# Turning m and x1 to features with 32x32 transposes on VectorE in place of TensorE transposes

## The chip, the cores and the metric

The kernel runs on one core of a Trainium2 chip. Its time is the device time of one execution in microseconds (us). The engines are named as in the profile: PE is TensorE (matmul), PEld its weight load, DVE is VectorE, ACT is ScalarE, POOL is GpSimd, and SP is SyncE, which only issues transfers here. Each engine works through a queue of its own in order; waits between engines go through semaphores.

## What is computed

The reference is one layer of a hybrid decoder block over 256 tokens with 2048 features, in float32. Cut to what matters here:

```python
h = rmsnorm(x, norm_mix_g)
u = h @ w_in                     # 12288 columns, split into ten fields
ya = ...                         # short convolution branch, from four fields
yb = ...                         # HGRN2 branch, from four fields
m = sigmoid(ga) * (ya @ w_a_out) + sigmoid(gb) * (yb @ w_b_out)
x = x + m @ w_o                  # called x1 below
gate = sigmoid(rmsnorm(x, ple_norm_g) @ w_ple_gate)
x = x + gate * (p @ w_ple_proj)
return rmsnorm(x, final_norm_g)
```

## The kernel before

**Products.** Every matrix product is made of steps. A step takes 256 rows of a weight for 512 output columns. It has 2 row blocks, 2 halves of 128 tokens, and 3 matmuls for each (lines 805 to 807): both operands are split into a rounded part (`hi`) and the rest (`lo`), and `hi*hi + hi*lo + lo*hi` is summed in PSUM. The operand with the tokens is stationary, so it must lie with its features on the partitions, and the result comes out with the tokens on the partitions. A result that feeds the next product must therefore be turned, from tokens on the partitions to features on the partitions. That is done for `m` and for `x1`, among others.

**Weights.** SP loads a weight tile `raw` of 128x2048, good for two steps, into one of three buffers (line 105). For each step ScalarE rounds it into `whi` (line 118), and VectorE writes the rest into `wlo` (line 119). Four pairs of `whi` and `wlo` exist until the last groups, and the program splits three steps ahead (`LEAD = 3`).

**Groups and their order.** A group is one block of 512 output columns. The order is: 16 groups of the branch fields; then for j = 0 to 3 the groups `ga`, `gb` (8 steps each), `A`, `B` (4 steps each); then `O` for j = 0 to 3 (8 steps each), called O0 to O3 below; then for j = 0 to 3 `PP` (1 step) and `PG` (8 steps). `mT` is the operand of `O`, `x1T` that of `PG`, and both are read in the order of their feature blocks, so that the blocks of j = 3 are needed in steps 6 and 7 of the group.

**Epilogues.** What follows a group is a generator. It is advanced once after each step, so that a `yield` moves what comes after it behind the next step in program order. The build then orders each engine's queue by its own planning, so that the queues differ somewhat from the program order. For this document:

- `ep_bb` (lines 543 to 557) ends a `B` group. VectorE multiplies `gb` by the PSUM result (line 547), POOL adds `ga` (line 548), and two steps later TensorE turns the 128x1024 tile in eight 128x128 transposes into two PSUM banks (`transposed`, lines 170 to 184). A step later ScalarE copies the banks to `mT`'s `hi` (line 556), and VectorE writes its `lo`, `ml` in the profile (line 557).
- `ep_o` (lines 559 to 591) ends an `O` group. VectorE adds the result to `xs`, the residual (line 564), ScalarE sums squares (line 565), TensorE turns the four feature blocks (line 576), and `put` (lines 147 to 157) writes `x1T`'s `hi` on ScalarE (line 154) and `lo`, `xl` in the profile, on VectorE (line 155).

**Memory.** `t4()` gives a tile of 128x1024 from a ring of eight or five buffers in the temporary pool of the phase: `tmp1`, then `tmp2` from the first `ga` on, then `tmp3`. `third_part` (lines 764 to 785) runs in group O0, after its sixth step: it closes `tmp2` and the pool of the branch results, opens `tmp3` in their place, and has SP load `xs` (line 772, two transfers), the final gain (line 775) and `pT` (line 778). A transfer into the new pool waits for the last use of what lay there. VectorE and ScalarE split `pT` in the same phase (lines 781 and 782, `pl`).

Of the kernel before, what the change touches and what calls it, by code (L numbers as in the profile page):

```python
# [10 lines left out]
F32 = mybir.dt.float32  # L11
F32R = mybir.dt.float32r
AF = mybir.ActivationFunctionType
ALU = mybir.AluOpType
PSUM = bass.MemoryType.PSUM

P = 128
T = 256
NT = T // P
# [5 lines left out]
CW = 512  # L25
# [14 lines left out]
PRM_GMIX, PRM_GPLE, PRM_GHG, PRM_LB, PRM_CONV = 0, 16, 32, 40, 48  # L40
# [5 lines left out]
def hybrid_kernel(ctx, tc, xT, x, pT, prm, gfin, masks, w_in, w_a, w_b, w_o, w_pg, w_pp, out):  # L46
    nc = tc.nc
# [22 lines left out]
    state = {"tmp": "tmp1"}  # L70
# [3 lines left out]
    def nm(s):  # L74
        uid[0] += 1
        return f"{s}_{uid[0]}"

    def t4(tag="t4", bufs=None):
        bufs = bufs or {"tmp1": 8, "tmp2": 5, "tmp3": 5}[state["tmp"]]
        return pools[state["tmp"]].tile([P, 1024], F32, tag=tag, bufs=bufs, name=nm(tag))  # L80

    def bank(tag):
        return ps.tile([P, CW], F32, tag=tag, bufs=4, name=nm(tag))

    def sc(n, tag="sc", bufs=12):
        return small.tile([P, n], F32, tag=tag, bufs=bufs, name=nm(tag))
# [39 lines left out]
    ident = const.tile([P, P], F32, name="ident")  # L126
# [13 lines left out]
    def gain(base, k):  # L140
        return prm_t[:, base + k : base + k + 1]
# [5 lines left out]
    def put(op, k, src, scale=None):  # L147

        hi, lo = op[0][:, k, :], op[1][:, k, :]
        if scale is None:  # L150
            nc.scalar.activation(out=hi, in_=src, func=AF.Copy)
            nc.vector.tensor_tensor(out=lo, in0=src, in1=hi.bitcast(F32), op=ALU.subtract)
        else:
            nc.scalar.activation(out=hi, in_=src, func=AF.Identity, scale=scale)
            nc.vector.scalar_tensor_tensor(
                out=lo, in0=src, scalar=scale, in1=hi.bitcast(F32), op0=ALU.mult, op1=ALU.subtract
            )


    def rsqrt_of(ss, n, width, tag):  # L160

        v = sc(n, tag + "v", 2)
        nc.vector.tensor_scalar(
            out=v, in0=ss, scalar1=1.0 / width, scalar2=EPS, op0=ALU.mult, op1=ALU.add
        )
        r = sc(n, tag + "r", 2)
        nc.gpsimd.tensor_tensor(out=r, in0=v, in1=mhalf[:, :n], op=ALU.pow)
        return r

    def transposed(src):  # L170

        banks = []
        for half in range(2):
            b = bank("s")
            for i in range(2):
                c = half * 2 + i
                for t in range(NT):
                    nc.tensor.transpose(  # L178
                        b[:, i * T + t * P : i * T + (t + 1) * P],
                        src[:, t * CW + c * P : t * CW + (c + 1) * P],  # L180
                        ident,
                    )
            banks.append(b)
        return banks


    def scaled(psum, dst):
# [26 lines left out]
    def ep_f(j, psum):  # L214
        fl = t4()
        scaled(psum, fl)
        yield
        bk = transposed(fl)
        yield
        sg, sn = t4(), t4()  # L220
# [43 lines left out]
    def ep_q(j, psum):  # L264
        sg, qt = t4(), t4()
        sig(psum, sg)
        times(psum, sg, qt)
        yield
        yield
        bk = transposed(qt)  # L270
        yield
        qT = t4("qT", 1)
        for h in range(2):
            nc.vector.tensor_copy(out=qT[:, h * 512 : (h + 1) * 512], in_=bk[h])
        state["qT", j] = qT
# [16 lines left out]
    def hgrn(j):  # L292
# [161 lines left out]
        yield  # L454
        yield
        bk = transposed(yb)
        yield
        for h in range(2):
# [84 lines left out]
    def ep_bb(j, psum):  # L543
        ga, gb = state["ga", j], state["gb", j]
        for t in range(NT):
            s = slice(t * CW, (t + 1) * CW)
            nc.vector.tensor_tensor(out=gb[:, s], in0=gb[:, s], in1=psum[t], op=ALU.mult)  # L547
        nc.gpsimd.tensor_tensor(out=gb, in0=ga, in1=gb, op=ALU.add)  # L548
        yield
        yield  # L550
        bk = transposed(gb)
        yield
        for h in range(2):
            k = j * 4 + h * 2
            hi, lo = (x[:, k : k + 2, :].rearrange("p k t -> p (k t)") for x in state["mT"])
            nc.scalar.activation(out=hi, in_=bk[h], func=AF.Copy)
            nc.vector.tensor_tensor(out=lo, in0=bk[h], in1=hi.bitcast(F32), op=ALU.subtract)

    def ep_o(j, psum):
        xs = state["x"]  # L560
        src = t4()
        for t in range(NT):
            d = xs[:, t, j * CW : (j + 1) * CW]
            nc.vector.tensor_tensor(out=d, in0=d, in1=psum[t], op=ALU.add)
            nc.scalar.activation(
                out=src[:, t * CW : (t + 1) * CW], in_=d, func=AF.Square,
                accum_out=state["ss2"][:, t * 4 + j : t * 4 + j + 1],
            )
        yield
        bk = []  # L570
        for half in range(2):
            b = bank("s")
            for i in range(2):
                c = j * 4 + half * 2 + i
                for t in range(NT):
                    nc.tensor.transpose(  # L576
                        b[:, i * T + t * P : i * T + (t + 1) * P], xs[:, t, c * P : (c + 1) * P], ident
                    )
            bk.append(b)
        yield  # L580
        for h in range(2):
            for i in range(2):
                k = j * 4 + h * 2 + i
                put(state["x1T"], k, bk[h][:, i * T : (i + 1) * T], gain(PRM_GPLE, k))
        if j == 3:
            tot = sc(2, "tot2", 1)
            nc.vector.tensor_reduce(
                out=tot, in_=state["ss2"].rearrange("p (t j) -> p t j", t=NT),
                axis=mybir.AxisListType.X, op=ALU.add,
            )  # L590
            state["rstd2"] = rsqrt_of(tot, NT, D, "r2")
# [64 lines left out]
    def ep_last(t, halves):  # L656
# [7 lines left out]
    epilogues = {  # L664
        "f": ep_f, "q": ep_q, "iv": ep_iv, "og": ep_og, "c": ep_c, "xa": ep_xa, "za": ep_za, "b": ep_b,
        "ga": ep_ga, "gb": ep_gb, "A": ep_a, "B": ep_bb, "O": ep_o, "PG": ep_pg, "PP": ep_pp,
    }
    groups = []
# [22 lines left out]
    for c in range(KT // 2):  # L691
        n = 2 * (c % 2)
        nc.sync.dma_start(
            out=xraw[c // 2].rearrange("p (k t) -> p k t", k=4)[:, n : n + 2, :],
            in_=xT[:, 2 * c : 2 * c + 2, :],
# [116 lines left out]
    for pos, (gi, c) in enumerate(steps[:last_group]):  # L812
        kind, j, w, g, opname = groups[gi]
# [25 lines left out]
        hi, lo = parts.pop(pos)  # L839
        for i in range(2):  # L840
            k = 2 * c + i
            s = slice(i * CW, (i + 1) * CW)
# [25 lines left out]
    for t, halves in ((0, (0, 1)), (1, (0,)), (1, (1,))):  # L868
        bk, n = bank("g"), CW // 2
        for c in range(nlast):  # L870
# [3 lines left out]
            hi, lo = parts[last_group + c]  # L874
            for i in range(2):
                k = 2 * c + i
                s = slice(i * CW + halves[0] * n, i * CW + (halves[-1] + 1) * n)
# [83 lines left out]
```

## Time and profile before

| what | value |
|---|---|
| median of 3 runs | 852.69 us (852.5 to 853.07) |
| the profiled execution | 852.66 us, of which its span is 850.9 us |
| granted TensorE clock in it | 0.998 |
| busy: PE, DVE, ACT, POOL | 839.6, 527.2, 425.0, 82.8 us |
| transferred | 164.12 MB, mean 193 GB/s |

How to read the rows. A row of a timeline has the start, the duration, the engine, the line, the operation, `out<-in`, the count of merged instructions, and in brackets how long the engine sat idle before it and what ended that. A row of a group has the count behind `x`, then the busy time in us and the mean duration in ns, then the idle time in front and its releasers. In the chain of waits a row has the start, the duration, the engine, the tile and the line. Matmuls are pipelined, so each shows 0.39 us but a new one starts every 0.227 us, and a busy PE isn't a PE at its peak. Times in the text are us unless ns is said.

### The profile page before, as it was taken

The numbers are of one execution on the slowest core, as the hardware profiler recorded it, in microseconds if no ns is written. First come the engines' busy times: TensorE is split into PE (matmuls) and PEld (weight loads), VectorE is DVE, ScalarE is ACT, GpSimd is POOL, SyncE is SP. The second block draws the span as 40 slices with busy tenths as digits, with TensorE's granted clock in tenths as the row PEclk, the third lists the DMA queues.
The fourth block names the chain that finished last, engine by engine and source line by source line (L and its number), as shares of the span: only waits on it lengthen the run. The fifth ranks groups of instructions, "written<-read, shape, count | busy, mean of one in ns | idle before, by whom it ended". The sixth has DMA issues, their size and how long they took to land.

```text
span 850.9 us, 9907 instructions
## 1 busy us (share of the span) xinstructions
PE 839.6 (99%) x3897; PEld 697.8 (82%) x3897; DVE 527.2 (62%) x611; ACT 425.0 (50%) x514; POOL 82.8 (10%) x76
## 2 busy tenths in 40 slices
PE   9999999999999999999999999999999999999995
PEld 6788888888888888888888888888888888888885
DVE  7484686977674587968446446446446555556572
ACT  7854664434644754534443444444444554455553
POOL 1010042202010042101001001001001000001110
PEclk9999999999999999999999999999999999999999
DMA  9865464444555455444555555555555955554542
GB/s 340 335 215 184 158 223 162 171 174 155 191 199 177 169 198 178 169 165 174 169 191 191 198 197 199 171 193 188 190 198 173 362 181 186 184 196 165 197 149 99
DMA packets 25966, 164.12 MB, mean 193 GB/s; under 512 B 3008, under 2 KB 3008, under 8 KB 7744
## 3 DMA queue, kind: packets, MB, share of 16 engines
q1 hardware_dynamic: 25488, 162.93, 53.8%
q8 instruction: 30, 0.49, 0.2%
q10 hardware_dynamic: 432, 0.56, 0.2%
q14 instruction: 16, 0.13, 0.0%
HBM read 161.39 MB, written 2.10 MB: 192 GB/s over the span
## 4 chain that ended last, share of the span: by engine, by line
PE 96%; issue 1%; DMA 1%; ACT 1%; DVE 0%; SPq 0%; POOLq 0%; POOL 0%; ACTq 0%
PE g L806 31%; PE g L807 31%; PE g L805 31%; PE s L310 1%; PE s L178 1%; DMA raw<-in_w_in 1%; PE s L418 0%; PE s L576 0%; PE s L430 0%; PE s L431 0%; PE s L429 0%; ACT whi L118 0%; ACT xs L647 0%; ACT t L630 0%; SPq L700 0%
## 5 line engine op out<-in xcount | busy, mean ns | idle before, releaser
L119 DVE TENSOR_TENSOR wlo<-raw,whi 128x1024 fp32r<-128x1024 f32 (+1 forms) x294 | 372.6, 1273 | 270.6 <-ACT whi L118 270.0
L118 ACT ACTIVATE whi<-raw 128x1024 fp32r<-128x1024 f32 (+1 forms) x294 | 308.6, 1053 | 361.9 <-PE g L807 354.4
L805 PE MATMUL g<-whi,xh 128*128 128x512 f32 (+1 forms) x912 | 354.5, 389 | 0.9 <-ACT whi L118 0.9
L806 PE MATMUL g<-wlo,xh 128*128 128x512 f32 (+1 forms) x912 | 352.0, 386 | 0.2 <-DVE wlo L119 0.2
L807 PE MATMUL g<-whi,xl 128*128 128x512 f32 (+1 forms) x912 | 351.8, 386 | 0.0
L805 PEld LDWEIGHTS g<-whi,xh 128*128 128x128 f32 x912 | 171.5, 188 | 35.5 <-ACT whi L118 2.3
L806 PEld LDWEIGHTS g<-wlo,xh 128*128 128x128 f32 x912 | 171.5, 188 | 34.8 <-DVE wlo L119 1.2
L807 PEld LDWEIGHTS g<-whi,xl 128*128 128x128 f32 x912 | 171.4, 188 | 34.4
L805 PE MATMUL g<-whi,mh 128*128 128x512 f32 x128 | 50.2, 392 | 0.0
L807 PE MATMUL g<-whi,ml 128*128 128x512 f32 x128 | 49.9, 390 | 0.0
L806 PE MATMUL g<-wlo,mh 128*128 128x512 f32 x128 | 49.8, 389 | 0.0
L548 POOL TENSOR_TENSOR gb<-ga,gb 128x1024 f32<-128x1024 f32 x4 | 9.6, 2396 | 258.3 <-DVE gb L547 258.3
L807 PEld LDWEIGHTS g<-whi,ml 128*128 128x128 f32 x128 | 24.0, 188 | 5.1
L806 PEld LDWEIGHTS g<-wlo,mh 128*128 128x128 f32 x128 | 24.0, 188 | 4.9
L805 PEld LDWEIGHTS g<-whi,mh 128*128 128x128 f32 x128 | 24.0, 188 | 4.8
L338 POOL TENSOR_TENSOR X<-t,kT 128x256 f32<-128x256 f32 x12 | 11.5, 956 | 168.3 <-ACT t L352 115.4
L805 PE MATMUL g<-whi,yaTh 128*128 128x512 f32 x64 | 24.9, 389 | 0.0
L806 PE MATMUL g<-wlo,yaTh 128*128 128x512 f32 x64 | 24.9, 389 | 0.0
L807 PE MATMUL g<-whi,yaTl 128*128 128x512 f32 x64 | 24.9, 389 | 0.0
L805 PE MATMUL g<-whi,ybTh 128*128 128x512 f32 x64 | 24.9, 389 | 0.0
L806 PE MATMUL g<-wlo,ybTh 128*128 128x512 f32 x64 | 24.9, 389 | 0.0
L807 PE MATMUL g<-whi,ybTl 128*128 128x512 f32 x64 | 24.9, 389 | 0.0
(153 smaller groups left out, 559.1 us busy)
## 6 DMA issues: line engine op xcount, KB each, us to landing
raw<-in_w_in SPq DMA_DIRECT2D x91, 1024.0 KB, 4.8
raw<-in_w_o SPq DMA_DIRECT2D x16, 1024.0 KB, 4.8
raw<-in_w_pg SPq DMA_DIRECT2D x16, 1024.0 KB, 4.7
raw<-in_w_a SPq DMA_DIRECT2D x8, 1024.0 KB, 5.0
raw<-in_w_b SPq DMA_DIRECT2D x8, 1024.0 KB, 5.0
raw<-in_w_in SPq DMA_DIRECT2D x9, 512.0 KB, 7.8
t<-in_xT SPq DMA_DIRECT2D x8, 256.0 KB, 7.0
t<-in_x SPq DMA_DIRECT2D x4, 512.0 KB, 8.7
```

Of the source, the lines that this page charges most:

```text
L118: nc.scalar.activation(out=hi[:, s], in_=src[:, s], func=AF.Copy)
L119: nc.vector.tensor_tensor(out=lo[:, s], in0=src[:, s], in1=hi[:, s].bitcast(F32), op=ALU.subtract)
L178: nc.tensor.transpose(b[:, i * T + t * P : i * T + (t + 1) * P], src[:, t * CW + c * P : t * CW + (c + 1) * P], ident,)
L310: nc.tensor.matmul(bk[:, s], X[:, 0, h, :], X[:, 1, h, :], start=True, stop=True)
L338: eng.tensor_tensor(out=xv[:, w, :, :, half, :], in0=ev[:, :, blk, :, half, :], in1=src[:, :, blk, :, half, :], op=ALU.mult,)
L548: nc.gpsimd.tensor_tensor(out=gb, in0=ga, in1=gb, op=ALU.add)
L805: nc.tensor.matmul(psum, oh, hi, start=first, stop=False)
L806: nc.tensor.matmul(psum, oh, lo, start=False, stop=False)
L807: nc.tensor.matmul(psum, ol, hi, start=False, stop=last)
```

## The change

VectorE can transpose blocks of 32x32 inside 32 partitions, and may write them to another quarter of the partitions. A new helper `turned` makes the whole turn of a 128x1024 tile in 16 such instructions, one for each pair of a source quarter `a` and a destination quarter `b`. Each handles 32 partitions and 2x4x32 elements. It yields after every `step` of them, 4 in general and 8 for the last x1 block. The result goes to an SBUF tile of the `t4` ring, not to PSUM, and the copies that follow read it there: for `m` one copy and one subtraction of 1024 columns in place of two of 512. The `tmp2` pool, which held only `ga` and `gb`, now holds the ring too.

```diff
+    def turned(src, dst, step):
...
+        s = src.rearrange("p t (c b e) -> p t c b e", b=4, e=32)
+        d = dst.rearrange("p c (t a e) -> p t c a e", t=NT, e=32)
+        for n in range(16):
+            a, b = n % 4, n // 4
+            nc.vector.transpose(
+                out=d[32 * b : 32 * b + 32, :, :, a, :], in_=s[32 * a : 32 * a + 32, :, :, b, :]
+            )
+            if n % step == step - 1:
+                yield
...
         nc.gpsimd.tensor_tensor(out=gb, in0=ga, in1=gb, op=ALU.add)
         yield
-        yield
-        bk = transposed(gb)
-        yield
-        for h in range(2):
-            k = j * 4 + h * 2
-            hi, lo = (x[:, k : k + 2, :].rearrange("p k t -> p (k t)") for x in state["mT"])
-            nc.scalar.activation(out=hi, in_=bk[h], func=AF.Copy)
-            nc.vector.tensor_tensor(out=lo, in0=bk[h], in1=hi.bitcast(F32), op=ALU.subtract)
+        m = t4()
+        yield from turned(
+            gb.rearrange("p (t n) -> p t n", t=NT), m.rearrange("p (c n) -> p c n", c=4), 4
+        )
+        k = j * 4
+        hi, lo = (x[:, k : k + 4, :].rearrange("p k t -> p (k t)") for x in state["mT"])
+        nc.scalar.activation(out=hi, in_=m, func=AF.Copy)
+        nc.vector.tensor_tensor(out=lo, in0=m, in1=hi.bitcast(F32), op=ALU.subtract)
...
         yield
-        bk = []
-        for half in range(2):
-            b = bank("s")
-            for i in range(2):
-                c = j * 4 + half * 2 + i
-                for t in range(NT):
-                    nc.tensor.transpose(
-                        b[:, i * T + t * P : i * T + (t + 1) * P], xs[:, t, c * P : (c + 1) * P], ident
-                    )
-            bk.append(b)
-        yield
-        for h in range(2):
-            for i in range(2):
-                k = j * 4 + h * 2 + i
-                put(state["x1T"], k, bk[h][:, i * T : (i + 1) * T], gain(PRM_GPLE, k))
+        x1 = t4()
+        yield from turned(xs[:, :, j * CW : (j + 1) * CW], x1.rearrange("p (c n) -> p c n", c=4), 8 if j == 3 else 4)
+        for c in range(4):
+            put(state["x1T"], j * 4 + c, x1[:, c * T : (c + 1) * T], gain(PRM_GPLE, j * 4 + c))
```

## The prediction

> **What bounds the kernel now.** I read the busy shares and the chain of waits first, then the groups of instructions.
>
> ```profile
> span 850.9 us, 9907 instructions
> PE 839.6 (99%) x3897; PEld 697.8 (82%) x3897; DVE 527.2 (62%) x611; ACT 425.0 (50%) x514; POOL 82.8 (10%) x76
> PE 96%; issue 1%; DMA 1%; ACT 1%; DVE 0%; SPq 0%; POOLq 0%; POOL 0%; ACTq 0%
> L119 DVE TENSOR_TENSOR wlo<-raw,whi 128x1024 fp32r<-128x1024 f32 (+1 forms) x294 | 372.6, 1273 | 270.6 <-ACT whi L118 270.0
> L118 ACT ACTIVATE whi<-raw 128x1024 fp32r<-128x1024 f32 (+1 forms) x294 | 308.6, 1053 | 361.9 <-PE g L807 354.4
> ```
>
> TensorE is 96% of the chain. VectorE waits for ScalarE, and ScalarE waits for TensorE to give a weight buffer back. So whatever leaves TensorE shortens the run, as long as VectorE's `wlo` stays ahead of the matmuls.
>
> The PE timeline around the first transposes of `gb` gives the rhythm.
>
> ```profile
> 453.31 0.39 PE L805 MATMUL g<-whi,xh 128*128 128x512 f32 x1
> 456.03 0.39 PE L805 MATMUL g<-whi,xh 128*128 128x512 f32 x1
> 458.76 1.04 PE L178 MATMUL s<-ident,gb 128*128 128x128 f32 x8
> 459.55 0.47 PE L805 MATMUL g<-whi,xh 128*128 128x512 f32 x1
> 462.39 0.39 PE L805 MATMUL g<-whi,xh 128*128 128x512 f32 x1
> ```
>
> A step (256 weight rows, 12 matmuls) takes 456.03 - 453.31 = 2.72. From 456.03 to 462.39 there are two steps and eight transposes: 6.36 - 5.44 = 0.92 for one block of eight. The chain of waits lists eight such blocks, first and last here:
>
> ```profile
> 458.92 0.87 PE s L178 x8
> ...
> 745.56 0.87 PE s L576 x8
> ```
>
> **The change part by part.** Removed: 64 TensorE transposes in 8 blocks, all on the chain: 8 x 0.92 = 7.4 us.
>
> Added: 128 VectorE transposes of 32 partitions x 256 elements (2x4x32), 16 per block. No row shows one. The nearest rows are instructions with 256 elements per partition, and for the far end the scan:
>
> ```profile
> L234 DVE TENSOR_SCALAR kT<-t,lc 128x256 f32<-128x256 f32 x8 | 2.7, 346 | 0.0
> L408 DVE TENSOR_TENSOR kT<-kT,t 128x256 f32<-128x256 f32 x4 | 1.7, 416 | 0.0
> L155 DVE SCALAR_TENSOR_TENSOR xl<-s,prm_t,xh 128x256 fp32r<-128x256 f32 x16 | 7.1, 479 | 0.6 <-ACT xh L154 0.3
> 679.83 0.87 DVE L155 SCALAR_TENSOR_TENSOR xl<-s,prm_t,xh 128x256 fp32r<-128x256 f32 x2
> L253 DVE TENSOR_TENSOR_SCAN b<-carry,t 128x1024 f32<-128x1024 f32 x2 | 4.6, 2284 | 0.0
> ```
>
> Lower end: two L155 take 0.87 for 2 x 0.479, so neighbours overlap by 0.09; 0.45 less that is 0.36. Upper end, a transpose that moves as slowly as the scan: L408 and the 1.23 of `wlo` (below) give 1.06 ns per element and 0.145 fixed, so the scan needs (2284 - 145) / 1024 = 2.09 ns per element, and 256 elements 0.68. I take T = 0.45 without overlap, between L408 and L155: one pass of 256 elements with a little to fill. The range keeps 0.36 and 0.68.
>
> The rows show overlap only between instructions on all 128 partitions. The Trainium skill (VectorE: DVE Perf Modes, Two Vector instructions with no wait between them) says that an instruction whose input or output starts in another quarter of the partitions than the one before is held until all earlier ones have finished, and here the input quarter changes every time; with overlap the total would be 845.3, held 846.8 (both below), and no row can show which. The same page (The three transpose paths) gives 311 ns for a 128x128 bf16 VectorE transpose; 128 elements more at 0.96 GHz make an estimate of 0.44, and by it 846.5.
>
> Now, does VectorE stay ahead? The first block, with 0 at 453.31:
>
> ```profile
> 453.51 1.06 ACT L118 ACTIVATE whi<-raw 128x1024 fp32r<-128x1024 f32 x1 [1.66 <-PE g L807]
> 453.02 1.28 DVE L547 TENSOR_TENSOR gb<-gb,g 128x512 f32<-128x512 f32 x2
> 454.38 2.39 POOL L548 TENSOR_TENSOR gb<-ga,gb 128x1024 f32<-128x1024 f32 x1 [66.76 <-DVE gb L547]
> 454.60 3.25 DVE L119 TENSOR_TENSOR wlo<-raw,whi 128x1024 fp32r<-128x1024 f32 x1 [0.30 <-ACT whi L118]
> 460.05 1.23 DVE L119 TENSOR_TENSOR wlo<-raw,whi 128x1024 fp32r<-128x1024 f32 x1 [1.06 <-ACT whi L118]
> 461.19 1.28 DVE L557 TENSOR_TENSOR ml<-s,mh 128x512 fp32r<-128x512 f32 x2
> 466.41 1.23 DVE L119 TENSOR_TENSOR wlo<-raw,whi 128x1024 fp32r<-128x1024 f32 x1 [1.49 <-ACT whi L118]
> ```
>
> Weights have four buffers, so the `wlo` made at 454.60 is read three steps later, at 3 x 2.72 + 0.23 = 8.39; the k-th after it at 8.39 + 2.72k. Per step VectorE has 1.49 idle, which hides three transposes. The changed program's queue runs wlo0, 5T, wlo1, 5T, wlo2, 5T, wlo3, T, wlo4, ml. The first transpose waits for POOL's add (end 3.46), but wlo0 already ends at 4.54, because it takes 3.25 beside that add; nothing is queued behind the wait that is not covered. With 1.25 per `wlo`: wlo1 ends at 8.05 (due 11.1), wlo2 at 11.55 (due 13.8), wlo3 at 15.05 (due 16.55), wlo4 at 16.75 (due 19.3), ml at 18.0. Least spare: 1.5. No stall. If the cover went, each 0.1 of T would cost 1.5 a block.
>
> The copies cost nothing: the two L557 of 1.28 become one of some 1.25, two ScalarE copies become one of 1.06 like `whi`, and the scalings of x1 read SBUF, where ScalarE's form takes 494 ns against 468:
>
> ```profile
> L154 ACT ACTIVATE xh<-t,prm_t 128x256 fp32r<-128x256 f32 x16 | 7.2, 494 | 0.3 <-DMA t<-in_xT 0.3
> L154 ACT ACTIVATE xh<-s,prm_t 128x256 fp32r<-128x256 f32 x16 | 6.8, 468 | 3.8 <-DVE xl L155 3.8
> ```
>
> ScalarE's 1.66 idle per step hides it.
>
> Moved: the load of x for the residual (L772). It goes where `tmp2` lay, and `tmp2` now holds `m`. In the changed queue it stands behind two more loads of `w_o`, the second of which waits for wlo4, and it waits itself for the last `ml`. Before:
>
> ```profile
> 651.93 0.39 PE L805 MATMUL g<-whi,mh 128*128 128x512 f32 x1
> 656.95 1.61 SPq L772 DMA_DIRECT2D xs<-in_x  x2
> DMA to landing us min/median/max: 8.1/8.7/9.4
> 659.08 0.43 SPq L778 DMA_DIRECT2D t<-in_pT  x1
> DMA to landing us min/median/max: 11.6/11.6/11.6
> 674.19 0.69 DVE L564 TENSOR_TENSOR xs<-xs,g 128x512 f32<-128x512 f32 x1 [1.90 <-issue]
> 673.27 1.06 ACT L118 ACTIVATE whi<-raw 128x1024 fp32r<-128x1024 f32 x1 [1.93 <-DMA raw<-in_w_o]
> DMA to landing us min/median/max: 3.2/4.8/13.2
> ```
>
> (The three landing rows are of x, of pT, and of all weight loads.) With 0 at O's first matmul (651.93), x was issued at 5.0 and landed 9.3 later, well before its first use at 674.19 - 651.93 - 0.92 = 21.3. Now it is issued at 18.0 (ml, above). The `w_o` load ahead of it leaves 1.25 earlier than x, so I take a landing at 26.9 (26.4 to 27.3): 5.6 too late, and VectorE waits in front of its queue: add, wlo8, add, wlo9, 8T, pl, wlo10, 5T, wlo11, 3T, wlo12, four xl, wlo13. From 26.9, an add 0.6: wlo8 28.75 (due 30.15), wlo9 30.6 (32.87), 8T 34.2, pl 34.8 (pT lands at 18.0 + 2.1 + 11.6 = 31.7), wlo10 36.05 (due 35.59, late 0.46), wlo11 39.55 (due 38.31, late 1.24), wlo12 42.15 (due 42.27 by then), xl 44.05, wlo13 45.3 (due 44.99): 0.31 more. TensorE stalls 1.24 + 0.31 = 1.55 here, once. The loads queued behind x shift with it: the first weight load after it was in at 673.27, 16.3 after x's issue, so now at 34.3, and its `whi` at 35.4, ahead of wlo11's start at 38.3; gfin is first read in the last phase.
>
> The other x1 blocks have x. Group O3, whose queue holds T, wlo0, 7T, wlo1, 8T, wlo2, four xl, wlo3:
>
> ```profile
> 742.39 1.28 DVE L564 TENSOR_TENSOR xs<-xs,g 128x512 f32<-128x512 f32 x2
> 743.97 1.23 DVE L119 TENSOR_TENSOR wlo<-raw,whi 128x1024 fp32r<-128x1024 f32 x1 [0.30 <-ACT whi L118]
> ```
>
> The adds end 1.0 after its last step: wlo0 2.7, wlo1 7.1 (due 11.1), wlo2 11.95 (13.8), wlo3 15.15 (16.55): 1.4 to spare; x1 is read six steps into PG0, after PP0's one, at 19. O1 and O2, with a `wlo` in every five transposes, keep 3.8.
>
> Sum against the profiled execution's own 852.66 us (1.76 outside the span; the median is 852.69): 852.66 - 7.4 + 1.55 = 846.8.
>
> **The rivals.**
>
> Full gain: T 0.36 by overlap, or x early by 1.6: the stall goes (1.55 - 31 x 0.09 is below nothing) and 845.3 follows. For it: L155's overlap. Against: no row has it across quarters.
>
> Slower: VectorE becomes the bound, because a float32 transpose costs two passes, like the scan. At T = 0.68 each of four m blocks loses 15 x 0.23 - 1.5 = 1.95, the O0 block 1.55 + 31 x 0.23 - 1.95 = 6.7 (B3's own loss pays part), O3 16 x 0.23 - 1.4 = 2.3, O1 and O2 nothing: 16.8 - 7.4 = +9.4, 862.1. It decides from T = 0.58, where m loses 4 x 0.45, O0 5.1 and O3 0.7, 7.6 in all. For it: no transposing instruction is in the trace; against: every plain 256-element row is at most 0.48.
>
> No change: x lands 13.2 after issue, as the latest weight load did, at 31.2: 4.3 more on a `wlo` that is late already. 846.8 + 4.3 = 851.1. For it: gfin, pT and weights share the queue; against: x's own 9.4.
>
> **How the numbers follow.** Forecast 0.50 (T from 0.41 to 0.54: 846 to 850), full gain 0.16, no change 0.07, slower 0.27. This kernel's runs tell 0.2% (1.7 us) from no change, so faster 0.66, same 0.07, slower 0.27. The range 845 to 858 goes up to T = 0.63 and leaves out the upper part of the slower case, towards 862.1.
>
> **What would show it.** A transpose row of 0.4 to 0.5 starting where the last one ends; no idle PE time in ga, gb, A and B steps; the x adds waiting for their load in O0, then some 1.5 of PE waiting for `wlo` in O1; PE's last matmul some 6 us earlier. Wrong if a transpose takes over 0.58, if PE waits in the m blocks, or if x's issue stays near 5.

## The result, and the profile after

| | us, median | range |
|---|---|---|
| before | 852.66 | 852.5 to 853.07 |
| after | 847.41 | 847.35 to 847.55 |

The ratio is 0.9938 [0.9919, 0.9958]: 0.6% faster, 5.25 us. One more execution of the changed kernel took 4834.85 us, with its 128x512 matmuls 1.28 to 1.46 us apart at a granted clock of 1.00, for a reason that isn't known, and the profile of that set fell on it; so the profile read here is that of a second set of the same kernel (847.24, 846.72 to 847.41; its profiled execution 846.72, the fastest of the four).

First the page of the changed kernel: the span, the busy times, the chain of waits by engine, and the two groups that prepare the weights.

```profile
span 844.9 us, 9887 instructions
PE 832.2 (98%) x3833; PEld 690.6 (82%) x3833; DVE 580.4 (69%) x735; ACT 423.8 (50%) x510; POOL 86.0 (10%) x76
PE 94%; DVE 2%; issue 2%; DMA 1%; ACT 1%; SPq 0%; POOLq 0%; POOL 0%; ACTq 0%
L119 DVE TENSOR_TENSOR wlo<-raw,whi 128x1024 fp32r<-128x1024 f32 (+1 forms) x294 | 371.6, 1272 | 207.1 <-ACT whi L118 205.5
L118 ACT ACTIVATE whi<-raw 128x1024 fp32r<-128x1024 f32 (+1 forms) x294 | 307.4, 1052 | 330.8 <-PE g L812 315.7
```

PE is busy 7.4 less, and DVE 53.2 more, which came out of its idle time in front of `wlo` (270.6 before, 207.1 now). But the chain shows something new: DVE holds 2% of it, where it had 0%. So somewhere TensorE waited for VectorE. The groups of transposes and a DVE timeline of the block behind B0 come next.

```profile
L196 DVE STREAM_TRANSPOSE t<-xs 32x256 f32<-32x256 f32 x64 | 27.9, 436 | 1.1
L196 DVE STREAM_TRANSPOSE t<-gb 32x256 f32<-32x256 f32 x64 | 27.9, 436 | 1.0
```

```profile
454.30 3.25 DVE L119 TENSOR_TENSOR wlo<-raw,whi 128x1024 fp32r<-128x1024 f32 x1 [0.30 <-ACT whi L118]
457.48 2.22 DVE L196 STREAM_TRANSPOSE t<-gb 32x256 f32<-32x256 f32 x5
459.73 1.22 DVE L119 TENSOR_TENSOR wlo<-raw,whi 128x1024 fp32r<-128x1024 f32 x1
460.99 2.23 DVE L196 STREAM_TRANSPOSE t<-gb 32x256 f32<-32x256 f32 x5
...
469.67 1.23 DVE L573 TENSOR_TENSOR ml<-t,mh 128x1024 fp32r<-128x1024 f32 x1
```

A transpose takes 436 ns, and five in a row 2.22: (2.22 - 0.436) / 4 = 0.446 from start to start, so none begins before the last one ends. VectorE has no idle time left in the block. Where TensorE waited is found with the busy time of PE by stretches (start to end, length, PE busy, matmuls, granted clock, DMA share and GB/s): the first three rows hold the first three `m` blocks, the fourth is O0, the fifth O1, and the sixth holds O2, O3 and most of the `PP` and `PG` groups.

```profile
452.00:520.00 68.00, 68.00 (x302) 1.00 0.57 199
520.00:580.00 60.00, 60.00 (x267) 1.00 0.56 193
580.00:640.00 60.00, 60.00 (x266) 1.00 0.56 193
648.85:671.94 23.09, 22.31 (x97) 1.00 0.53 192
671.94:693.70 21.76, 21.76 (x97) 1.00 0.78 302
693.70:820.00 126.30, 126.30 (x559) 1.00 0.54 194
```

PE idles in O0 alone. Before, it had no idle time there either, eight transposes included:

```profile
651.93:674.60 22.67, 22.67 (x105) 1.00 0.80 313
```

After, PE's timeline in O0, and VectorE's:

```profile
664.94 0.39 PE L812 MATMUL g<-whi,ml 128*128 128x512 f32 x1
665.54 0.50 PE L810 MATMUL g<-whi,mh 128*128 128x512 f32 x1 [0.21 <-ACT mh L572]
665.88 0.40 PE L811 MATMUL g<-wlo,mh 128*128 128x512 f32 x1
666.84 0.50 PE L812 MATMUL g<-whi,ml 128*128 128x512 f32 x1 [0.57 <-DVE ml L573]
667.18 0.40 PE L810 MATMUL g<-whi,mh 128*128 128x512 f32 x1
```

```profile
663.95 0.44 DVE L196 STREAM_TRANSPOSE t<-gb 32x256 f32<-32x256 f32 x1
664.42 1.23 DVE L119 TENSOR_TENSOR wlo<-raw,whi 128x1024 fp32r<-128x1024 f32 x1
665.57 1.22 DVE L573 TENSOR_TENSOR ml<-t,mh 128x1024 fp32r<-128x1024 f32 x1
666.70 2.35 DVE L119 TENSOR_TENSOR wlo<-raw,whi 128x1024 fp32r<-128x1024 f32 x2
670.58 1.22 DVE L119 TENSOR_TENSOR wlo<-raw,whi 128x1024 fp32r<-128x1024 f32 x1 [1.52 <-ACT whi L118]
674.25 0.69 DVE L580 TENSOR_TENSOR xs<-xs,g 128x512 f32<-128x512 f32 x1 [2.45 <-DMA xs<-in_x]
...
676.72 0.69 DVE L580 TENSOR_TENSOR xs<-xs,g 128x512 f32<-128x512 f32 x1 [0.65 <-DMA xs<-in_x]
677.33 1.22 DVE L119 TENSOR_TENSOR wlo<-raw,whi 128x1024 fp32r<-128x1024 f32 x1
```

And SP's, where the load of x is issued:

```profile
666.87 0.80 SPq L777 DMA_DIRECT2D xs<-in_x  x2
```

The matmuls that wait are the first of O0's step 6, which reads the last `m` block. The last transpose ends at 664.39, and step 6 was due at 665.17; `mh` came a little late and `ml` at 666.79. The starts in these rows are 0.60, 0.34, 0.96 and 0.34 apart in place of 0.227: 2.24 - 0.91 = 1.33 lost. The load of x came out as the forecast had it, issued 18.0 after O0's first matmul (666.87 - 648.85), and the adds wait for it; but O1, which was to pay, has no idle PE at all.

The profiled pair agrees with that: 852.66 - 7.36 + 1.33 = 846.63, and 846.72 was measured. Two other differences cancel in this. The profiled execution was 0.30 ahead before the first changed instruction (`wlo` at 454.30, before at 454.60), and its end behind PE's last matmul is 0.36 longer (844.9 - 835.67 against 850.9 - 842.03). A stretch that holds neither is the one from O0's first matmul to PE's last: 186.82, before 190.10, so 3.28 less. Five of the eight blocks lay in it, and 5 x 0.92 - 1.33 = 3.27.

### The profile page after: what moved, and what is told of

It reads as the page before. It is cut to its first block, busy times and chain, and to the rows that moved or that the text cites. A ratio compares the mean times of both kernels' runs of the same rounds, so it can differ in the third digit from the quotient of the medians.

```text
span 4833.0 us, 9887 instructions
## 1 busy us (share of the span) xinstructions
PE 4822.6 (100%) x3833; PEld 3387.5 (70%) x3833; DVE 583.7 (12%) x735; ACT 427.7 (9%) x510; POOL 77.2 (2%) x76
## 4 chain that ended last, share of the span: by engine, by line
PE 98%; issue 1%; ACT 0%; DVE 0%; POOLq 0%; POOL 0%
PE g L810 32%; PE g L812 31%; PE g L811 31%; PE s L326 2%; PE s L178 1%; PE s L434 0%; PE s L713 0%; PE s L445 0%; PE s L446 0%; PE s L447 0%; ACT xs L652 0%; ACT t L635 0%; DVE t L631 0%; POOLq L961 0%; POOL r L647 0%
## 5 line engine op out<-in xcount | busy, mean ns | idle before, releaser
L810 PE MATMUL g<-whi,xh 128*128 128x512 f32 (+1 forms) x912 | 1534.7, 1684 | 0.0
L811 PE MATMUL g<-wlo,xh 128*128 128x512 f32 (+1 forms) x912 | 1524.1, 1671 | 0.0
L812 PE MATMUL g<-whi,xl 128*128 128x512 f32 (+1 forms) x912 | 1523.9, 1671 | 0.0
L812 PEld LDWEIGHTS g<-whi,xl 128*128 128x128 f32 x912 | 833.3, 914 | 359.6 <-issue 359.6
L810 PEld LDWEIGHTS g<-whi,xh 128*128 128x128 f32 x912 | 834.6, 915 | 349.9 <-issue 348.9
L811 PEld LDWEIGHTS g<-wlo,xh 128*128 128x128 f32 x912 | 833.3, 914 | 348.5 <-issue 347.3
L810 PE MATMUL g<-whi,mh 128*128 128x512 f32 x128 | 216.9, 1695 | 0.0
L812 PE MATMUL g<-whi,ml 128*128 128x512 f32 x128 | 216.8, 1694 | 0.0
L811 PE MATMUL g<-wlo,mh 128*128 128x512 f32 x128 | 216.8, 1693 | 0.0
L812 PEld LDWEIGHTS g<-whi,ml 128*128 128x128 f32 x128 | 116.9, 913 | 52.5 <-issue 52.5
```

What stands on the lines that cost most here:

```text
L810: nc.tensor.matmul(psum, oh, hi, start=first, stop=False)
L811: nc.tensor.matmul(psum, oh, lo, start=False, stop=False)
L812: nc.tensor.matmul(psum, ol, hi, start=False, stop=last)
```

## The experiments

Before is measured beside each: 852.49 (`again` to `m_apart`), 852.54 (`m6` to `twice`), 852.39 (`halves`).

| label | what | us, median (range) | ratio to before [95%] |
|---|---|---|---|
| again | the change itself | 847.24 (846.72 to 847.41) | 0.994 [0.9924, 0.9955] |
| only_m | only m on VectorE | 852.85 (852.39 to 853.15) | 1.0003 [0.9994, 1.0012] |
| only_x1 | only x1 on VectorE | 848.72 (848.57 to 848.84) | 0.9956 [0.9944, 0.9969] |
| m_apart | m in a pool of its own | 847.45 (846.78 to 847.57) | 0.994 [0.9927, 0.9952] |
| m6 | last m block 6 per step | 848.07 (847.52 to 850.48) | 0.9954 [0.994, 0.9967] |
| m6_apart | both of these | 845.75 (845.51 to 846.23) | 0.992 [0.9907, 0.9932] |
| quarter | 20 transposes a block | 851.9 (851.31 to 852.47) | 0.9991 [0.9982, 1.0] |
| twice | 32 transposes a block | 901.46 (900.6 to 902.58) | 1.0573 [1.0559, 1.0588] |
| halves | m6_apart, each cut in two | 847.48 (one run) | one run each |

### The change as it is, and its two parts

> The changed kernel itself, for a profile. Two theories of why 847.4 us and not 845.3 (852.7 less eight blocks of 0.92): A, the load of x is late in group O0 and TensorE then waits for wlo once, in O1; B, a little is lost in each of the eight blocks, because sixteen transposes take more than VectorE has to spare. A expects transposes of 0.40 to 0.50 us each, the first x transfer issued 17 to 19 us after O's first matmul, VectorE idle in front of the x add of O0 until some 27 us after it, 1.5 to 2.2 us of waits of PE for wlo, all within 20 us after the end of O0, and none elsewhere. B expects transposes over 0.55 us and 0.2 to 0.3 us of PE waits in every block. Both expect 847.4 us.

The profile above has the transposes, the late x and the idle VectorE much as A had them, but the PE wait lies in O0 and is for `mh` and `ml`, which neither theory had.

`only_m` puts the old lines for x1 back, `only_x1` the old lines for m:

```diff
 # only_m, in ep_o
-        x1 = t4()
-        yield from turned(xs[:, :, j * CW : (j + 1) * CW], x1.rearrange("p (c n) -> p c n", c=4), 8 if j == 3 else 4)
+        bk = []
+        for half in range(2):
...
 # only_x1, in ep_bb
-        m = t4()
...
+        bk = transposed(gb)
```

> m is turned on VectorE, x1 on TensorE as before. By the sum four blocks give 4 x 0.92 = 3.7 us. A expects that x is still late (issued after the last ml, landed some 27 us after O's first matmul), and that the TensorE transposes of x1, which stand behind the first step of O1 (24.5 us after O's first matmul), wait for the x adds (ending near 29.4 us): a single PE wait of 4 to 5 us, and so 852.7 - 3.7 + 4.5 = 853.5 us (852.5 to 854.5). B expects 852.7 - 3.7 and half of the 2.1 us that are missing, 850.0 us.

> x1 is turned on VectorE, m on TensorE as before. A expects x as early as before the change (issued 5 us after O's first matmul), no wait of PE, and the full gain of four blocks: 852.7 - 3.7 = 849.0 us (848.7 to 849.3). B expects 850.0 us.

x1 alone gains 3.77, which is four blocks at 0.92 (3.68): its turn on VectorE costs nothing in time, and x is loaded early (issued at 656.73, 5.0 after O's first matmul) since `m` isn't in the way. m alone gains nothing. Its PE timeline shows the wait of O0 again, the same 0.21 for `mh` and 0.57 for `ml`, and then TensorE's own transposes of x1 waiting for the late x:

```profile
675.68 0.44 PE L592 MATMUL s<-ident,xs 128*128 128x128 f32 x2 [0.50 <-DVE xs L580]
678.14 0.88 PE L592 MATMUL s<-ident,xs 128*128 128x128 f32 x6 [1.32 <-DVE xs L580]
```

There x1 is turned on the engine that sets the end, so a late x stops it directly. From 674.57 to 679.32 seven matmuls start where 1.59 would do for them; less the 0.92 of an ordinary block, 4.75 - 1.59 - 0.92 = 2.24 are lost. A had put 4 to 5 on this one wait. With O0's 1.33: -3.68 + 1.33 + 2.24 = -0.11, measured +0.36. In the profiled execution PE's last matmul starts at 841.99, 0.04 ahead of before, and the end behind it is 9.31 long in place of 8.87. So the two gains do not simply add up (0 and 3.8, together 5.25): with x1 on VectorE too, the late x falls on an engine with time to spare.

### The late load of x alone, and the late ml alone

`m_apart` gives `m` memory that the load of x doesn't need. `m6` makes the last m block's transposes six to a step, so that they are through a step sooner. `m6_apart` does both.

```diff
 # m_apart, m6_apart
-        m = t4()
+        m = pools["m"].tile([P, 1024], F32, tag="mt", bufs=1, name=nm("mt"))
 # m6, m6_apart
-            gb.rearrange("p (t n) -> p t n", t=NT), m.rearrange("p (c n) -> p c n", c=4), 4
+            gb.rearrange("p (t n) -> p t n", t=NT), m.rearrange("p (c n) -> p c n", c=4), 6 if j == 3 else 4
```

> The changed kernel, but the tile with the turned m lies in the pool of mT, not in the ring of the pool that x replaces. A expects that the load of x no longer waits for the last ml but only for a second w_o load ahead of it (issued some 12 us after O's first matmul, landed by 21 us), no wait of PE for wlo, and the full gain: 845.3 us (845.0 to 845.8). B expects 847.4 us as for the changed kernel.

With `m` apart x is issued at 661.56, and both adds run without waiting. The time doesn't move: 847.45. The full gain that A expected of it did not come, since the wait for `ml` stands as before; B's number came, though not for B's reason. The rows are from SP's, VectorE's and PE's timelines of `m_apart`.

```profile
661.56 0.86 SPq L777 DMA_DIRECT2D xs<-in_x  x2
```

```profile
672.45 1.28 DVE L580 TENSOR_TENSOR xs<-xs,g 128x512 f32<-128x512 f32 x2
```

```profile
666.26 0.50 PE L810 MATMUL g<-whi,mh 128*128 128x512 f32 x1 [0.21 <-ACT mh L572]
666.60 0.40 PE L811 MATMUL g<-wlo,mh 128*128 128x512 f32 x1
667.57 0.50 PE L812 MATMUL g<-whi,ml 128*128 128x512 f32 x1 [0.57 <-DVE ml L573]
```

> The changed kernel with 6 in place of 4 transposes per step for the last m block. The profile of the changed kernel shows one place where TensorE waits that is not in the forecast: 1.33 us in step 6 of O0, for mh and ml of the last m block. Theory M: this wait is the whole remaining loss, and the late x load costs nothing because this wait gives VectorE the time back. Theory X: the x load costs 1.5 us as in the forecast. M expects the last ml to end 16.7 us after O's first matmul in place of 18, no PE wait in O0, at most 0.4 us of PE waits for wlo in O1, and 847.2 - 1.2 = 846.0 us (845.5 to 846.5). X expects 847.2 us.

`m6` removes the wait in O0, and is no faster: 848.07 (847.52 in the profiled execution), above both expectations. Now O1 waits for `wlo`, as the forecast had said of the change itself. PE's, ScalarE's and VectorE's timelines of `m6`:

```profile
683.73 0.50 PE L811 MATMUL g<-wlo,mh 128*128 128x512 f32 x1 [1.59 <-DVE wlo L119]
```

```profile
679.13 2.01 ACT L118 ACTIVATE whi<-raw 128x1024 fp32r<-128x1024 f32 x2 [1.94 <-DMA raw<-in_w_o]
```

```profile
673.46 0.69 DVE L580 TENSOR_TENSOR xs<-xs,g 128x512 f32<-128x512 f32 x1 [1.77 <-DMA xs<-in_x]
...
677.93 4.49 DVE L196 STREAM_TRANSPOSE t<-xs 32x256 f32<-32x256 f32 x10
682.45 2.36 DVE L119 TENSOR_TENSOR wlo<-raw,whi 128x1024 fp32r<-128x1024 f32 x2
```

x still waits for `ml`, and one `w_o` load fewer is ahead of it: the load for O1's steps 4 and 5 now stands behind x, gfin and pT. So ScalarE waits 1.94 for that load before it makes `whi`, ten transposes go ahead of the `wlo` that needs it, and PE loses 1.87.

> As m6, and the turned m lies in the pool of mT, so that x is loaded before the last ml. M expects no PE wait for mh, ml or wlo in O0 and O1 and at most 0.4 us less than m6: 845.8 us (845.2 to 846.3). X expects the gain to come from here and not from m6: 845.5 us here against 847.2 us there.

With both edits O0 and O1 run without an idle PE, and the time is 845.75, the fastest of all: 6.8 below before. The loads stand in the order of `m6`, so what `m6` lost in O1 goes back to the late x (VectorE's queue differs too, by two transposes in front of one `wlo`).

```profile
649.15:670.91 21.76, 21.76 (x97) 1.00 0.57 223
670.91:692.67 21.76, 21.76 (x98) 1.00 0.79 304
```

PE's last matmul starts at 834.70, 7.33 ahead of before, which is the whole of eight times 0.92. From O0's first matmul it is 185.55, before 190.10: 4.55 less for the five blocks there (4.60), so no wait of any size is left. The end behind PE's last matmul is 0.4 longer (844.0 - 834.70 against 850.9 - 842.03). So it is in `again`, `only_m` and `m_apart`, where `m` is on VectorE too, and not in `only_x1` (846.9 - 838.07 = 8.83); the cause is open. The four kernels make a table: one edit alone gives nothing, both give 1.5.

| us | x behind ml | x early |
|---|---|---|
| last m block 4 per step | 847.24 | 847.45 |
| last m block 6 per step | 848.07 | 845.75 |

### The price of a transpose

Two kernels put more transposes into each block, and compute the same. `quarter` does one in four twice, `twice` does all of them twice (the same line with `range(2)`).

```diff
+            for _ in range(2 if a == 0 else 1):
                 nc.vector.transpose(
```

> The changed kernel with every fourth transpose done twice: 20 in place of 16 per block, 1.4 to 1.8 us more of VectorE. By the sum each block has 1.4 to 1.5 us to spare for wlo, so the first three m blocks and O1 to O3 lose 0.3 us at most each, and only the last m block passes it on in full (ml later by 1.4 to 1.8 us) and the first x1 block 0.5 us: 2.4 to 3.0 us more, 849.9 us. If VectorE had nothing to spare, 8 x 1.6 us more: 860 us. If the spare were several us, 847.2 us.

> The changed kernel with every transpose done twice in a row: 32 per block, each pair with the same quarters. If an instruction with the same quarters as the one before overlaps with it, and only a change of quarter holds it back, a pair takes 0.80 us (0.36 + 0.44) and not 0.89. By the queues the first three m blocks then lose 3.2 us each, the last m block 8.2, the first x1 block 4, O1 and O2 2 each, O3 4.4: 30 us over the full gain of 845.1, 875 us. Without overlap in a pair 40 us, 885 us. If VectorE did not become the bound: 847 to 850 us.

`quarter` has 20 x 0.446 in a block, as if T were 0.56, and ends at 851.9, 2 above what was expected and 0.6 below before: it is close to the break-even that the forecast put at T = 0.58. The first three m blocks still cost PE nothing. O0 loses 3.2, O1 0.8, and PG0 1.6, a place that no expectation had named:

```profile
668.14 0.50 PE L811 MATMUL g<-whi,mh 128*128 128x512 f32 x1 [2.07 <-ACT mh L573]
...
756.09 0.50 PE L812 MATMUL g<-wlo,xh 128*128 128x512 f32 x1 [1.29 <-DVE wlo L119]
```

In PG0 VectorE still carries a delay from O2: it reaches O3's adds with no idle time before them.

`twice` was far slower than either expectation, and settles nothing on overlap: eight transposes take 3.65, 0.46 from start to start, so none overlaps, but the second of a pair writes the first one's output again and may have to wait for that, which no run shows. In the first m block PE waits 0.39, 1.91 and 0.36 for `wlo`. Most of what lies between 885 and 901 is the clock. The same two stretches in `twice` and in the change itself:

```profile
469.00:472.00 3.00, 1.53 (x7) 1.00 0.75 309
472.50:475.50 3.00, 3.00 (x8) 0.53 0.00 0
```

```profile
469.00:472.00 3.00, 3.00 (x15) 1.00 0.41 109
472.50:475.50 3.00, 3.00 (x15) 1.00 0.81 279
```

Behind the wait of 1.91 the granted clock is about one half for 3.4 us (472.44 to 475.85), and a matmul starts every 0.43. Over the whole run the clock is 0.980 against 0.996: 0.016 x 898.5 = 14 us.

### Does a change of quarter hold the next transpose?

`halves` takes `m6_apart` and cuts each transpose into two that follow each other with the same quarters.

```diff
-            nc.vector.transpose(
-                out=d[32 * b : 32 * b + 32, :, :, a, :], in_=s[32 * a : 32 * a + 32, :, :, b, :]
-            )
+            for t in range(NT):
+                nc.vector.transpose(
+                    out=d[32 * b : 32 * b + 32, t, :, a, :], in_=s[32 * a : 32 * a + 32, t, :, b, :]
+                )
```

> The kernel of m6_apart with every transpose cut into two of 32x128 elements that follow each other with the same quarters (32 instead of 16 per block). Theory H: VectorE starts an instruction early only when its quarters are those of the one before. Then, with 1.04 ns per element and 0.436 us for 256, a half takes 0.30 us, the second of a pair starts some 0.08 to 0.09 before the first has ended (0.22 after its start) and the next pair 0.31 later: 0.53 per pair, 8.5 us per block. Theory N: transposes never overlap on this engine, whatever their quarters. Then they start uniformly every 0.31 and a pair takes 0.62, 9.9 us per block. If the cost is all fixed, a half takes 0.44 as a whole does and a block 14 us. The total is above m6_apart's 845.75 by what passes the spare of the m blocks (1.5 us): some 846 to 849 by H, 849 to 856 by N.

The group, the durations of the first two in B0's block (ns, minimum, median and maximum), and the start of that block cut off after 2, 3, 4 and 5 of them (one row from each of four stretches that begin alike):

```profile
L197 DVE STREAM_TRANSPOSE mt<-gb 32x128 f32<-32x128 f32 x128 | 32.7, 284 | 1.1
```

```profile
L197 DVE STREAM_TRANSPOSE mt<-gb x2: 258/275/292, 458.5 to 458.7; 32x128 f32<-32x128 f32 x2
```

```profile
458.51 0.49 DVE L197 STREAM_TRANSPOSE mt<-gb 32x128 f32<-32x128 f32 x2
458.51 0.80 DVE L197 STREAM_TRANSPOSE mt<-gb 32x128 f32<-32x128 f32 x3
458.51 0.99 DVE L197 STREAM_TRANSPOSE mt<-gb 32x128 f32<-32x128 f32 x4
458.51 1.30 DVE L197 STREAM_TRANSPOSE mt<-gb 32x128 f32<-32x128 f32 x5
```

Each step of this series is the distance between two ends. It goes 0.31, 0.19, 0.31. The first half lasts 0.292. The second lasts 0.258 and ends at 0.49, so it starts at 0.23, 0.06 before the first has ended. The third, from another quarter, lasts 0.299 and ends at 0.80, so it starts at 0.50, after the end of the second. That is theory H. A pair takes 0.50 to 0.51, more than the 0.446 of a whole transpose. A half that doesn't overlap the one before takes 0.30 against 0.436, as the expectation had it: (436 - 300) / 128 = 1.06 ns per element. The total, 847.48, lies in H's span, but N's begins at 849 and a single run would not part them; the rows do.

## Why the prediction was right, and where it was not

**The gain.** Eight blocks at 0.92: shown by `only_x1` (3.77 for four) and by PE's last matmul in `m6_apart` (7.33 for eight).

**T.** 0.45 without overlap was taken, 0.446 was measured. It lay between the rows of 416 and 479 ns, as argued; the overlap of the full-gain rival does exist (0.06 in `halves`), but only between neighbours of one quarter, which the change doesn't have. This is what the Trainium skill says (VectorE: DVE Perf Modes, Two Vector instructions with no wait between them), and `halves` agrees with it: 0.19 and 0.31 between the ends of neighbours. From the 311 ns of the Trainium skill (the same page, The three transpose paths) for 128x128 in bf16 an estimate of 0.44 had been worked out; 0.436 was measured, for 32x256 in float32.

**The m blocks.** A spare of 1.5 over 15 transposes was to cover T up to 0.55 or so. No PE time is lost in the first three blocks, nor in `quarter`, whose mean of 0.56 goes just to the edge.

**The load of x.** Issue at 18.0 behind the last `ml`: 18.0 measured. The sum took one landing for both transfers, 8.9 after issue. They land 7.3 and 9.4 after it, and the first add needs only the first: it starts at 25.4 instead of 26.9.

**The step that failed** is "TensorE stalls 1.24 + 0.31 = 1.55 here, once". It did not stall in O1 at all. Two things put it right by a little. With x earlier the last transpose-laden `wlo` of that place, the forecast's wlo11, ends at 38.6 after O0's first matmul (687.43 - 648.85) instead of 39.55, against 38.31 when it is due: late by 0.3, not by 1.24. And TensorE had by then been held up for 1.33 in O0, which moved every due time in O1 back by as much.

**What stood in its place** is a wait that the forecast had the numbers for and did not compare. It put the `ml` of a block at 18.0 from the block's first matmul, checked each `wlo` against its due time, and did not check `ml` itself. For j = 0 to 2 `mT` is read much later; for j = 3 the next group is O0, whose step 6 starts at 6 x 2.72 = 16.3 and reads `ml` 0.45 later, at 16.8. 18.0 - 16.8 = 1.2 would have been its price by the forecast's own terms; 1.33 was measured. So 846.8 came out right with a stall of nearly the same size, one group earlier and from another wait: 1.33 for 1.55. That the two sizes are so near is luck: the place and the wait were others than forecast. `m_apart` shows that the late x isn't what costs here, `m6` that it does once the wait for `ml` is gone (1.87 there, with a weight load moved behind x; by the due times of the change itself it would be the 0.3 above), and `m6_apart` that nothing else is left.

**The rivals.** The full gain (845.3) is what `m6_apart` reaches, 845.75, by another way than overlap: `ml` ahead of step 6 and x early together. No change by a late landing: x landed in 9.4 at the most, not 13.2. Slower from T = 0.58: `quarter` nearly bears the threshold out, since at its mean of 0.56 the forecast's terms give 1.6 below before and 0.6 was measured. The price far above it came out too low, since the halved clock that `twice` shows was in none of the terms.

**Signs that were named.** The row of 0.4 to 0.5, the quiet ga, gb, A and B steps, the x adds waiting for their load and PE's end some 6 earlier were there; the 1.5 of PE waiting for `wlo` in O1 was not.

## What to carry to other kernels

When work moves to an engine that runs just ahead of the one that sets the end, compare the end of every result in its queue with the moment at which it is read, the last one's above all: the result that the whole sequence was for was late here, while every weight between had been checked. Two waits in a row can cover each other, so that removing either one alone gives nothing, as here, and only both together give the gain. Look up, too, what memory a new tile shares: a transfer that waits for its last use moves with it, and so does everything behind that transfer in its queue.

## What the hardware did that was not expected

Behind a wait of PE of about 2 us its granted clock can fall to half for 3.4 us (`twice`, 0.53 from 472.5 to 475.5). It does not always follow. Of seven PE waits between 1.76 and 1.97 us in `twice`, four have matmuls 0.42 to 0.43 apart at once or a few matmuls later, and three do not; all three longer ones (3.45, 5.64 and 6.50) have them. In `quarter` PE waits 2.07 in O0, and the granted clock behind it stays at 1.00 (668.2 to 671.6). What decides wasn't tried. The Trainium skill (TensorE: Matmul & The Clock Gate, Part 1: The HAM clock gate) tells of a clock that is halved after an idle window of some 3.4 us, in windows that run freely; the 3.4 us at half speed agree, but PE's wait of 1.91 before them is shorter than such a window.
